# The order of the first column chunks of a fused input projection, and the place of two loads

## The chip, the cores and the metric

One core of one Trainium2 chip. The metric is the device time of one execution in microseconds (us). A core has TensorE (PE in the profile; its weight loads are PEld), VectorE (DVE), ScalarE (ACT), GpSimd (POOL) and SyncE (SP), and 16 DMA engines that serve the queues of SP and POOL. Each engine works through its own instructions in order.

## The reference

One layer of a decoder trunk in float32 with 256 tokens and model width 2048. Three sub-layers, each followed by a LayerNorm of the scaled residual: a hybrid token mixer, a cross-attention into 256 memory tokens, and a SwiGLU feed-forward network. The change lies in the mixer:

```python
gdn_qkv, gdn_gate, gdn_beta, gdn_alpha, ret_qkvg, rwkv_in = jnp.split(x @ w_in, IN_SPLITS, axis=-1)
y_a = gated_deltanet(...)
y_b = retention(...)
y_c = rwkv7_time_mix(rwkv_in, ...)
y = jnp.concatenate([y_a, y_b, y_c], axis=-1)
return y @ w_out
```

and in it in the RWKV-7 group, 12 heads of 64:

```python
p = p + (p_prev - p) * mu                      # token shift
r, k, v, wd, ad, gd = jnp.split(p, RWKV_SPLITS, axis=-1)
w_log = -jax.nn.softplus(-(w0 + jnp.tanh(wd) @ w_up)) - 0.5
decay = jnp.exp(-jnp.exp(w_log))
a = jax.nn.sigmoid(a0 + ad @ a_up)
g = jax.nn.sigmoid(gd) @ g_up
kk = l2_normalize(heads(k * k_k))
k = k * (1.0 + (a - 1.0) * k_a)
...                                            # S_t = S_{t-1}(diag(w) - kk^T (kk a)) + v k^T, y_t = S_t r_t
return y.reshape(b, t, h * n) * g
```

The RWKV part of `w_in` has 2560 columns: 768 of r, 768 of k, 768 of v, and 256 of the rates' inputs (wd, ad, gd).

## The kernel before

Every large product is made by `gemm`. It goes over column chunks of the weight matrix; for each it loads the 2048 rows in four pieces of 512 rows (`ws`, two buffers, issued on SP at line 171), and splits each piece into a high and a low part, two k tiles at a time: a cast on ACT (`wh`, line 181) and a subtraction on DVE (`wl`, line 182). Each k tile then takes six products on PE (lines 159 to 161, for two blocks of 128 tokens: high by high, high by low, low by high). After the last k tile the chunk goes to a `consume` function, here `take`. The parameter `before` lets `load_x` bring the input x in during the first chunk: it loads 512 columns of x on SP (line 260, four buffers), transposes them on PE (line 138) and splits them the same way.

After each k tile, `gemm` calls `hook`, which is the object `side`: a set of lanes (generators). A lane does a piece of work and yields the number of hook calls after which it goes on. So the side work of RWKV, then of the gated DeltaNet group and of retention, is placed between the products. A scheduler in the build then orders each engine's instructions from this program order and from priorities. Lanes wait for each other by flags (`side.until`).

The program begins with the RWKV projection, in seven chunks: the 256 columns of the rates first, then two chunks of 384 for k, two for r and two for v. `take` evacuates each: copies to `nat` (line 389), PE transposes (`wt`, line 399), copies into `buf` (443) and the token shift on DVE (445, 447). For the rates it then applies tanh and sigmoid and adds the lane `from_keys`. That lane first makes the decays of both halves (`decays`, products `lr` at line 486, a scan at 498), then the keys of both halves (`keys`, from line 510, each half as soon as its flag `k0` or `k1` is up), then runs `delta`: the products `aab` into `AT` (line 601), the inverse of 24 triangular systems (`invert`: transposes at 313, a loop of 31 steps of two DVE instructions at 321 and 323, then transposes, copies and small products), with the scores (line 630, which copy under the mask `mask3` at 632) between, and the rest of the recurrence. `from_r` and `from_v` are lanes of their own, added when a chunk of r or v is evacuated; `from_r` sets the flag `r0` or `r1`, which the scores wait for, and ends in the products `pn` (line 406). After the seven chunks `side.run` calls the lanes until both halves of v are done; what is left of `delta` goes on between the products of the next projection, eight chunks of 384 or 396 columns for the gated DeltaNet group.

Small loads are issued on POOL's queue at the start: constants (`twoh`), `mask3` (192 KB), seven small parameter loads into `prow`, then `g_up` (384 KB) and the two halves of `wa_up` (192 KB each). `mask3` is read first by the scores, `g_up` by the products at line 746, near the end of `delta`. At the end of `delta`'s first allocation POOL clears a part of `AT` (line 594).

Of the kernel before, what the change touches and what calls it, by code (L numbers as in the profile page):

```python
# [19 lines left out]
P = 128  # L20
D = 2048
T = 256
NB = T // P
# [8 lines left out]
WH, WN = 12, 64  # L32
WW = WH * WN
# [7 lines left out]
C_RWKV = C_RET + 4 * RW  # L41
# [55 lines left out]
def tile_kernel(ctx: ExitStack, tc: tile.TileContext, ap: dict, out: bass.AP, dbg=None):  # L97
    nc = tc.nc
# [9 lines left out]
    def pst(name):  # L108
        return pm.tile([P, 512], F32, tag="t", name=name, bufs=2)
# [163 lines left out]

    C = load_consts(p1, "twoh", "twoh")
    mask3 = p1.tile([P, 3 * P], I32, tag="mask3", name="mask3")
    nc.gpsimd.dma_start(mask3, ap["mask3"])
    prow = p1.tile([P, P], F32, tag="prow", name="prow")
    nc.vector.memset(prow, 0.0)
    PR_MU, PR_W0, PR_A0, PR_KK, PR_KA, PR_RK, PR_CONV = 0, 20, 26, 32, 38, 44, 50
# [6 lines left out]
    def transpose_params():  # L286
        pp_ = pst("pp")
        nc.tensor.transpose(pp_[:, :P], prow, ident)
        nc.scalar.copy(prm, pp_[:, :P])

    def par(row, j):
        return prm[:, row + j:row + j + 1]
# [88 lines left out]
    HC = WCT // 2  # L381
    G = WH // 2

    def evac_transposed(ps, n, put):

        nat = []
        for b in range(NB):
            t = p1.tile([P, 384], F32, tag="nat", name="nat", bufs=4)
            nc.scalar.copy(t[:, :n], ps[b][:, :n])
            nat.append(t)  # L390
        transposed([t for t in nat], n // P, put)

    def transposed(nat, nt, put, js=None):
        for j in js if js is not None else range(0, nt, 2):
            w = min(2, nt - j)
            pt = pst("wt")
            for i in range(w):
                for b in range(NB):
                    nc.tensor.transpose(pt[:, i * T + b * P:i * T + b * P + P], nat[b][:, (j + i) * P:(j + i + 1) * P], ident)  # L399
            put(j, w, pt[:, :w * T].rearrange("p (i t) -> p i t", t=T))  # L400
# [13 lines left out]
    def rwkv(ctx2):  # L414
# [8 lines left out]
        nc.vector.memset(eps[:, 0:1], 1e-12)  # L423
        nc.vector.memset(eps[:, 1:2], 64e-5)
        g_up = wp.tile([P, WW], F32, tag="gup", name="gup")
        nc.gpsimd.dma_start(g_up, ap["rwkv_g_up"][0])
        gdt = wp.tile([P, T], F32, tag="gdt", name="gdt")

        wl = ctx3.enter_context(tc.tile_pool(name="wl", bufs=1, reuse_waits="tile"))
# [9 lines left out]
        def shifted(dsts, ct0):  # L439
            def put(j, w, pt):  # L440
                buf = wr.tile([P, 2, T + 1], F32, tag="buf", name="buf", bufs=2)
                nc.gpsimd.memset(buf[:, :, 0:1], 0.0)
                nc.scalar.copy(buf[:, :w, 1:], pt)
                d = wr.tile([P, 2, T], F32, tag="dsh", name="dsh", bufs=1)
                nc.vector.tensor_sub(d[:, :w], buf[:, :w, 0:T], buf[:, :w, 1:])
                for i in range(w):
                    nc.vector.scalar_tensor_tensor(dsts[j + i], d[:, i, :], par(PR_MU, ct0 + j + i), buf[:, i, 1:], ALU.mult, ALU.add)
            return put
# [12 lines left out]
        def take(ci, n, ps, bs):  # L461
            if ci == 0:
                transpose_params()
                evac_transposed(ps, n, shifted([wad, gdt], 3 * WCT))
                nc.scalar.activation(wad[0:64], wad[0:64], AF.Tanh)
                nc.scalar.activation(gdt, gdt, AF.Sigmoid)
                side.add(from_keys())
                return
            which, hf = order[ci - 1]
            t = wr.tile([P, HC, T], F32, tag=f"rkv{which}", name=f"rkv{which}", bufs=2 if which == 1 else 1)  # L470
            evac_transposed(ps, n, shifted([t[:, i] for i in range(HC)], which * WCT + hf * HC))
            if which == 1:
                key[hf] = t
                side.flag(f"k{hf}")
            else:
                side.add((from_r if which == 0 else from_v)(hf, t))
# [69 lines left out]
        def from_keys():  # L546
            yield 1
            yield from decays(0)
            yield from decays(1)
            for hf in range(2):  # L550
                yield from side.until(f"k{hf}")
                yield from keys(hf)
            ctx3.close()
            yield from delta(ctx2, RA, KB, vn, bon, fx, eps, g_up, gdt)
# [25 lines left out]
                yield 1  # L580
            side.flag(f"v{hf}")

        order = [(1, 0), (1, 1), (0, 0), (0, 1), (2, 0), (2, 1)]
        chunks = [(C_RWKV + 3 * WW, 256)] + [(C_RWKV + i * WW + hf * HC * P, HC * P) for i, hf in order]
        gemm(xT, w_in, chunks, take, before=load_x, hook=side)
        side.run("v0", "v1", "b0", "b1")
        ctxw.close()

    def delta(ctx2, RA, KB, vn, bon, fx, eps, g_up, gdt):
# [1 line left out]

        ws_ = ctx2.enter_context(tc.tile_pool(name="ws_", bufs=1, reuse_waits="tile"))
        AT = ws_.tile([P, 32, P], F32, tag="AT", name="AT")
        nc.gpsimd.memset(AT[:, NB * WH:, :], 0.0)
        for b in range(NB):
            for c0 in (0, 3):
                pts = [pst("aab") for _ in range(2)]
# [435 lines left out]
    def retention(ctx2):  # L1033
# [67 lines left out]
        for b in range(NB):  # L1101
# [9 lines left out]
            nc.vector.tensor_mul(y_b[:, b], y_b[:, b], yn)  # L1111

    rwkv(ctx.enter_context(ExitStack()))
    ctxr = ExitStack()
    rawp = ctxr.enter_context(tc.tile_pool(name="rawp", bufs=1, side="right", reuse_waits="tile"))
# [219 lines left out]
    with ExitStack() as c2:  # L1335
# [16 lines left out]
        chunks = []  # L1352
# [39 lines left out]
```

## Time and profile before

| | |
|---|---|
| runs shown | 1759.27, 1766.21, 1766.76 us (median 1766.21) |
| profiled execution | 1768.92 us, of which the profiled span 1767.1 us |
| busy share of PE, DVE, ACT, POOL | 98%, 59%, 46%, 4% |
| mean granted TensorE clock | 0.989 of full speed |
| HBM read, rate over the span | 300.63 MB, 171 GB/s |
| mask load, issue to landing | 6.3 us |
| g_up load, issue to landing | 6.0 us |
| first pieces of `ws`, 512 KB, issue to landing (median) | 6.9 us |

The table gives the whole execution. The busy share of PE contains products that run at a lower granted clock and products that wait inside a pipelined stretch, so a stage must also be read by its length against the number of products in it. Row views by window give, for each engine, busy us and the number of instructions, then the granted clock, the busy share of the DMA engines and GB/s. A row of the timeline gives start, length, engine, line, operation, output and inputs, and in brackets the idle time before it and what ended it.

### The profile page before, as it was taken

What the parts mean: (1) busy time and instruction counts of PE and PEld (TensorE: products, weight loads), DVE (VectorE), ACT (ScalarE), POOL (GpSimd) and SP (SyncE); (2) the same over time, 40 slices, a digit from 0 to 9 for tenths busy, and PEclk for the clock granted to TensorE, in tenths of its full rate; (3) what the DMA queues carried; (4) which work ended last, traced back from release to release, by engine and by line L of the source; (5) the groups of instructions that cost most, each with busy time, mean ns of one, the idle gap of its engine ahead of it and who ended that gap; (6) DMA issues with size and microseconds to landing.
All of it is one profiled execution on the core that took longest, in us unless ns stands there. A gap on an engine that the chain in (4) does not pass through costs nothing.

```text
span 1767.1 us, 22057 instructions
## 1 busy us (share of the span) xinstructions
PE 1726.0 (98%) x8853; PEld 1438.1 (81%) x8853; DVE 1035.8 (59%) x1473; ACT 806.8 (46%) x1087; POOL 64.8 (4%) x89
## 2 busy tenths in 40 slices
PE   7999999999999999999999999999999999999997
PEld 6878899898788788877888778888888888888885
DVE  4779357675489655566555755544445554444445
ACT  5633536764444454345543544444444444333342
POOL 2010010000000000011000110000000000000000
PEclk9979999999999999999999999999999999999999
DMA  6433235555544535745445555555555555555553
GB/s 208 144 108 108 92 110 164 161 191 177 180 167 167 190 121 177 273 169 191 143 144 167 188 193 191 190 191 191 190 190 186 187 187 185 185 190 190 191 190 120
DMA packets 158006, 304.15 MB, mean 172 GB/s; under 512 B 5449, under 2 KB 36226, under 8 KB 157136
## 3 DMA queue, kind: packets, MB, share of 16 engines
q1 hardware_dynamic: 156800, 300.01, 50.2%
q0 software_dynamic: 1104, 2.74, 0.6%
q8 instruction: 69, 1.13, 0.3%
q14 instruction: 33, 0.27, 0.0%
HBM read 300.63 MB, written 2.10 MB: 171 GB/s over the span
## 4 chain that ended last, share of the span: by engine, by line
PE 86%; DVE 9%; ACT 2%; issue 1%; DMA 1%; POOL 0%; ACTq 0%; DVEq 0%; POOLq 0%
PE g L159 26%; PE g L160 25%; PE g L161 25%; DVE wl L182 3%; ACT wh L181 1%; PE pt L127 1%; DMA ws<-in_w_in_dram 1%; DVE solX L323 1%; DVE solT L321 1%; DVE res L1238 1%; PE pt L138 1%; DVE solL L313 1%; PE wt L399 1%; PE py L754 1%; PE pn L406 0%
## 5 line engine op out<-in xcount | busy, mean ns | idle before, releaser
L182 DVE TENSOR_TENSOR wl<-ws,wh 128x1024 fp32r<-128x1024 f32 (+2 forms) x560 | 653.0, 1169 | 613.6 <-ACT wh L181 612.9
L181 ACT CAST wh<-ws 128x1024 fp32r<-128x1024 f32 (+2 forms) x560 | 559.5, 1003 | 729.8 <-PE g L161 638.9
L161 PE MATMUL g<-wh,x2T 128*128 128x512 f32 x692 | 271.4, 392 | 0.0
L159 PE MATMUL g<-wh,x2T 128*128 128x512 f32 x692 | 269.7, 390 | 0.0
L160 PE MATMUL g<-wl,x2T 128*128 128x512 f32 x692 | 269.6, 390 | 0.0
L159 PE MATMUL g<-wh,xT 128*128 128x384 f32 (+3 forms) x608 | 219.3, 361 | 0.8 <-ACT wh L181 0.8
L160 PE MATMUL g<-wl,xT 128*128 128x384 f32 (+3 forms) x608 | 217.0, 357 | 0.0
L161 PE MATMUL g<-wh,xT 128*128 128x384 f32 (+3 forms) x608 | 214.3, 352 | 0.0
L160 PEld LDWEIGHTS g<-wl,x2T 128*128 128x128 f32 x692 | 129.9, 188 | 27.3
L159 PEld LDWEIGHTS g<-wh,x2T 128*128 128x128 f32 x692 | 130.1, 188 | 26.4
L161 PEld LDWEIGHTS g<-wh,x2T 128*128 128x128 f32 x692 | 129.9, 188 | 26.1
L161 PE MATMUL g<-wh,hT 128*128 128x512 f32 x336 | 133.1, 396 | 0.0
L159 PE MATMUL g<-wh,hT 128*128 128x512 f32 x336 | 132.9, 396 | 0.0
L160 PE MATMUL g<-wl,hT 128*128 128x512 f32 x336 | 132.9, 395 | 0.0
L159 PEld LDWEIGHTS g<-wh,xT 128*128 128x128 f32 x608 | 117.2, 193 | 10.9 <-issue 2.6
L160 PEld LDWEIGHTS g<-wl,xT 128*128 128x128 f32 x608 | 117.2, 193 | 10.8 <-issue 4.2
L161 PEld LDWEIGHTS g<-wh,xT 128*128 128x128 f32 x608 | 117.1, 193 | 6.4 <-issue 1.5
L159 PE MATMUL g<-wh,mT 128*128 128x512 f32 x256 | 104.8, 409 | 0.0
L160 PE MATMUL g<-wl,mT 128*128 128x512 f32 x256 | 100.5, 393 | 1.6 <-DVE wl L182 1.6
L161 PE MATMUL g<-wh,mT 128*128 128x512 f32 x256 | 100.6, 393 | 0.0
L160 PEld LDWEIGHTS g<-wl,hT 128*128 128x128 f32 x336 | 63.2, 188 | 15.2
L161 PEld LDWEIGHTS g<-wh,hT 128*128 128x128 f32 x336 | 63.2, 188 | 15.2
(450 smaller groups left out, 2157.7 us busy)
## 6 DMA issues: line engine op xcount, KB each, us to landing
ws<-in_ffn_gate_up_dram SPq DMA_DIRECT2D x88, 1024.0 KB, 4.8
ws<-in_ffn_down_dram SPq DMA_DIRECT2D x44, 1024.0 KB, 5.0
ws<-in_w_in_dram SPq DMA_DIRECT2D x52, 768.0 KB, 4.2
ws<-in_w_in_dram SPq DMA_DIRECT2D x16, 1024.0 KB, 4.9
ws<-in_xattn_v_dram SPq DMA_DIRECT2D x16, 1024.0 KB, 5.0
ws<-in_xattn_k_dram SPq DMA_DIRECT2D x16, 1024.0 KB, 5.0
ws<-in_w_out_dram SPq DMA_DIRECT2D x16, 1024.0 KB, 5.1
ws<-in_xattn_q_dram SPq DMA_DIRECT2D x16, 1024.0 KB, 5.0
```

What stands on the lines that cost most here:

```text
L127: nc.tensor.transpose(pt[:, (n % 2) * P:(n % 2 + 1) * P], src(kt), ident)
L138: nc.tensor.transpose(pt[:, k * T + b * P:k * T + b * P + P], src(b, 2 * g + k), ident)
L159: nc.tensor.matmul(ps[b][:, :n], xh, wh, start=(k == 0), stop=False)
L160: nc.tensor.matmul(ps[b][:, :n], xh, wl, start=False, stop=False)
L161: nc.tensor.matmul(ps[b][:, :n], xl, wh, start=False, stop=(k == nk - 1))
L181: nc.scalar.copy(wh[:, :, :n], ws[:, 2 * k2:2 * k2 + 2, :n])
L182: nc.vector.tensor_sub(wl[:, :, :n], ws[:, 2 * k2:2 * k2 + 2, :n], wh[:, :, :n].bitcast(F32))
L313: nc.vector.transpose(L[p], at[p, :, p].rearrange("p s t -> p t s"))
L321: nc.vector.tensor_tensor(t, X[:, m:m + 1, 0:nj].to_broadcast([P, ni, nj]), L[:, m + 1:32, m:m + 1].to_broadcast([P, ni, nj]), ALU.mult)
L323: nc.vector.tensor_tensor(X[:, m + 1:32, 0:nj], X[:, m + 1:32, 0:nj], t, ALU.add)
L399: nc.tensor.transpose(pt[:, i * T + b * P:i * T + b * P + P], nat[b][:, (j + i) * P:(j + i + 1) * P], ident)
L754: nc.tensor.matmul(o, l, r, start=(start and n == 0), stop=(stop and n == len(ops) - 1))
```

## The change

The order of the first two chunks is exchanged: 384 columns of k (first half) come first, with x's loads beside them, and the 256 columns of the rates second. In `take`, the transposition of the parameter rows stays with the first chunk, the rates' evacuation and the start of the lane `from_keys` go to the second. The loads of `mask3` and `g_up` are no longer issued at the start but on POOL's queue directly behind the clearing of `AT` in `delta`; `tc.issue_after` fixes that order on the queue.

```diff
     mask3 = p1.tile([P, 3 * P], I32, tag="mask3", name="mask3")
-    nc.gpsimd.dma_start(mask3, ap["mask3"])
...
         g_up = wp.tile([P, WW], F32, tag="gup", name="gup")
-        nc.gpsimd.dma_start(g_up, ap["rwkv_g_up"][0])
...
         def take(ci, n, ps, bs):
             if ci == 0:
                 transpose_params()
+            if ci == 1:
                 evac_transposed(ps, n, shifted([wad, gdt], 3 * WCT))
                 nc.scalar.activation(wad[0:64], wad[0:64], AF.Tanh)
                 nc.scalar.activation(gdt, gdt, AF.Sigmoid)
                 side.add(from_keys())
                 return
-            which, hf = order[ci - 1]
+            which, hf = order[ci]
...
-        order = [(1, 0), (1, 1), (0, 0), (0, 1), (2, 0), (2, 1)]
-        chunks = [(C_RWKV + 3 * WW, 256)] + [(C_RWKV + i * WW + hf * HC * P, HC * P) for i, hf in order]
+        order = [(1, 0), None, (1, 1), (0, 0), (0, 1), (2, 0), (2, 1)]
+        chunks = [(C_RWKV + x[0] * WW + x[1] * HC * P, HC * P) if x else (C_RWKV + 3 * WW, 256) for x in order]
...
-        nc.gpsimd.memset(AT[:, NB * WH:, :], 0.0)
+        with tc.issue_after(nc.gpsimd.memset(AT[:, NB * WH:, :], 0.0).ins):
+            nc.gpsimd.dma_start(mask3, ap["mask3"])
+            nc.gpsimd.dma_start(g_up, ap["rwkv_g_up"][0])
```

## The prediction

> **What bounds the kernel now.** I read the page first: how busy TensorE (PE) is, and where in the span its share or its clock falls. 40 slices of a 1767 us span are 44.2 us each.
>
> ```profile
> span 1767.1 us, 22057 instructions
> PE 1726.0 (98%) x8853; PEld 1438.1 (81%) x8853; DVE 1035.8 (59%) x1473; ACT 806.8 (46%) x1087; POOL 64.8 (4%) x89
> PE   7999999999999999999999999999999999999997
> PEclk9979999999999999999999999999999999999999
> ```
>
> PE is the bound; only the first slices are thinner, and only the third shows a low clock. The change lives there, in the RWKV input projection. I cut that stretch where its seven column chunks end (each is 96 products of lines 159 to 161; I call the chunks c0 to c6) and add the first chunk after it. Columns: busy time of each engine, granted clock, DMA share, GB/s.
>
> ```profile
> 0.00:25.28 25.28, 17.93 (x129) 17.26 (x129) 10.77 (x20) 10.60 (x18) 9.22 (x24) 1.00 0.83 260
> 25.28:55.32 30.04, 26.36 (x127) 21.59 (x126) 16.92 (x29) 21.26 (x37) 0.10 (x1) 0.89 0.43 141
> 55.32:77.34 22.02, 21.33 (x116) 18.38 (x114) 17.64 (x29) 13.73 (x21) 0.28 (x2) 1.00 0.45 144
> 77.34:106.23 28.89, 28.81 (x140) 24.74 (x138) 20.46 (x30) 10.91 (x18) 5.12 (x5) 0.82 0.34 109
> 106.23:136.07 29.84, 26.01 (x135) 22.43 (x134) 23.29 (x35) 10.68 (x19) 3.06 (x5) 0.83 0.33 106
> 136.07:163.62 27.55, 26.96 (x183) 22.62 (x182) 25.80 (x56) 8.84 (x14) 0.20 (x2) 1.00 0.35 113
> 163.62:187.05 23.43, 22.41 (x207) 20.54 (x206) 21.14 (x41) 12.72 (x21) 0.20 (x2) 1.00 0.43 139
> 187.05:204.50 17.45, 17.45 (x262) 15.82 (x262) 4.40 (x7) 9.70 (x19) 0.00 (x0) 1.00 0.15 47
> ```
>
> Then the timeline of the start and of c1, for the pace of products and the waits inside "busy".
>
> ```profile
> 2.29 0.59 POOL L276 DMA_DIRECT2D mask<-in_mask_dram  x1
> 8.88 0.56 POOL L426 DMA_DIRECT2D gup<-in_rwkv_g_up_dram  x1 [0.88 <-DMA mask<-in_mask_dram]
> 10.02 0.78 PE L159 MATMUL g<-wh,xT 128*128 128x256 f32 x2
> 17.98 1.14 ACT L181 CAST wh<-ws 128x512 fp32r<-128x512 f32 x2 [2.90 <-DMA ws<-in_w_in_dram]
> 20.08 0.28 PE L159 MATMUL g<-wh,xT 128*128 128x256 f32 x1
> 20.20 0.28 PE L160 MATMUL g<-wl,xT 128*128 128x256 f32 x1
> 24.71 1.57 ACT L181 CAST wh<-ws 128x768 fp32r<-128x768 f32 x2 [3.57 <-DMA ws<-in_w_in_dram]
> 26.60 0.33 PE L399 MATMUL wt<-ident,nat 128*128 128x128 f32 x1 [1.20 <-ACT nat L389]
> 27.29 0.35 PE L159 MATMUL g<-wh,xT 128*128 128x384 f32 x1
> 27.47 0.34 PE L160 MATMUL g<-wl,xT 128*128 128x384 f32 x1
> 32.92 0.77 PE L486 MATMUL lr<-wad,waup 64*128 64x256 f32 x4 [1.15 <-ACT wad L465]
> 35.74 1.46 PE L486 MATMUL lr<-wad,waup 64*128 64x256 f32 x4 [1.33 <-ACT sg L488]
> 126.59 1.86 PE L406 MATMUL pn<-rkv,csts_twoh 128*6 128x256 f32 x4 [3.83 <-DVE rkv L565]
> ```
>
> Products start 0.12 us apart at 256 columns and 0.17 to 0.18 at 384, so a 384 chunk is worth about 16.6 us and a 256 chunk 11.5. The table shows c1 to c6 at 22 to 30 us: the RWKV side work and waits behind it take the rest. The granted clock falls three times there:
>
> ```profile
> 36.00:40.00 4.00, 4.00 (x12) 2.30 (x12) 0.80 (x2) 1.84 (x5) 0.00 (x0) 0.53 0.61 195
> 40.00:44.00 4.00, 4.00 (x16) 4.00 (x16) 3.42 (x9) 2.42 (x3) 0.00 (x0) 0.61 0.01 2
> 92.00:100.00 8.00, 8.00 (x29) 6.20 (x28) 6.15 (x9) 0.83 (x1) 1.23 (x2) 0.64 0.52 182
> 100.00:108.00 8.00, 8.00 (x45) 7.07 (x44) 1.64 (x2) 4.37 (x10) 3.64 (x2) 0.72 0.00 0
> 124.00:132.00 8.00, 5.41 (x15) 2.94 (x16) 6.54 (x17) 0.53 (x2) 0.00 (x0) 0.56 0.61 197
> 132.00:140.00 8.00, 8.00 (x41) 7.47 (x39) 5.06 (x11) 4.22 (x7) 0.00 (x0) 0.80 0.10 22
> ```
>
> By one minus the clock, times the window, these dips cost 3.4, 5.1 and 5.1 us.
>
> **The change, part by part.**
>
> *Loads taken from the start.* The mask (192 KB) and g_up (384 KB) go: 0.59 MB. The DMA engines move up to 374 GB/s there:
>
> ```profile
> 8.00:12.00 4.00, 2.71 (x13) 2.74 (x14) 2.48 (x4) 1.80 (x4) 1.92 (x7) 1.00 1.09 374
> ws<-in_w_in_dram SPq DMA_DIRECT2D x52, 768.0 KB, 4.2
> ```
>
> That is 1.6 us of DMA time. Removing both also takes two issues of 0.6 us off POOL's queue and lets the two loads of wa_up behind them go sooner.
>
> *A wider first chunk.* Each of its four weight loads grows from 512 to 768 KB, 0.26 MB or 0.7 us. The third load (its cast waits 2.90 us for it now) has 0.79 MB more and 0.59 less ahead of it: it lands 0.5 us later; the fourth 1.2 us later. Between first product and third load lie 48 products, 8.3 us instead of 5.8, so PE needs it 2.5 us later: covered, and the fourth too. The first product itself has no cover: load +0.7, cast and subtraction a half longer (1.14 us for two casts now, so about +0.3 each for one), mask's 0.5 us gone: between 0 and +1.3; I take +0.8.
>
> *The next chunk's loads.* Today c1's first cast waits 3.57 us for DMA, and PE 1.20 us for `nat`, a copy behind that cast on ACT. In the new order the 256-column loads are asked for while 384-column products still run (4.2 us per load against 24 x 0.173 = 4.15 us of products, two buffers). The wait goes: -1.2 (PE's own), bounds 0 and -3.6 (ACT's). What is late next is the same `nat` copy without DMA ahead of it.
>
> *Order of RWKV's side work.* I counted its steps (one per product pair of k). The decays start after the rates' chunk, now second: they move from c1 to c2, keys(0) from c2 to c3, keys(1) from the first ten steps of c3 to the end of c3 and five of c4; the inverse begins 11 steps later (c4 step 9, before c3 step 14), its 31-step loop ends at c6 step 16 instead of 5, and RWKV ends in the fourth instead of the third chunk of the next projection. That projection has 128 steps, and the group behind it ends at the same step in both orders. PE's side work is the same; what counts is what it lies beside. The waits of 1.15 and 1.33 us and the table loads behind them move with the decays: 0. Only the 256-column chunk now carries no decays.
>
> DVE decides c4 to c6 (25.80 of 27.55 us in c5). Rows of DVE's groups, first of the stretch 25 to 106, then 106 to 205:
>
> ```profile
> L182 DVE TENSOR_TENSOR wl<-ws,wh 128x768 fp32r<-128x768 f32 x27 | 25.4, 949 | 18.4 <-ACT wh L181 18.3
> ...
> L313 DVE STREAM_TRANSPOSE solL<-AT 32x1024 f32<-32x1024 f32 x4 | 8.1, 2018 | 2.0 <-ACT AT L604 1.9
> ...
> L331 DVE COPY AT<-AT 32x768 f32<-32x768 f32 x4 | 2.2, 546 | 0.1
> L326 DVE STREAM_TRANSPOSE solL<-solX 128x1024 f32<-128x1024 f32 x1 | 2.1, 2136 | 0.0
> L328 DVE STREAM_TRANSPOSE AT<-solX 128x1024 f32<-128x1024 f32 x1 | 2.0, 2003 | 0.0
> ```
>
> Eight weight subtractions are 7.6 us a chunk. c2 and c3 together hold 17.6 + 20.5 - 15.2 = 22.9 us of other DVE work, 11.4 for each half of the keys. New c3 gets one and a half halves: 7.6 + 17.1 = 24.7 us, against 22.0 us that c2 takes with 17.6 of DVE: +2.7. Out of c6 go the last transposes and copies, 2.1 + 2.0 + 2.2 = 6.3 us, into a chunk that has room (4.40 of 17.45); into c4 to c6 come half of the keys' work, about 5: -1.3. The wait of 3.83 us on `rkv`, behind transposes of 2.0 us each, should leave the r half that runs before them now and return at the second, which runs right after: 0, bounds -8.9 and +8.9 (wait and dip gone, or one of each added). Keys no longer needed the moment they arrive: -1 (0 to -2).
>
> *Mask and g_up later.* Issued behind POOL's clearing of AT, some ten steps before the scores read the mask: 0.59 MB beside weight loads at a DMA share of 0.33. Cost 0 to +1.6, I take +0.3. Queued behind them on POOL are only memsets of AT and `sc`, needed later still.
>
> *Dips.* Nothing removes their causes; they are short pauses whose timing shifts. Any of the three, 3.4 to 5.1 us, may go, or a fourth come. As c1 no longer combines late loads and decays, I count a third of a mean dip as gone: -1.5.
>
> Sum: +0.8 - 1.2 + 2.7 - 1.3 - 1 + 0.3 - 1.5 = -1.2; I round to -2 for POOL's and `wa_up`'s earlier issue. The profiled execution took 1768.9 (span plus 1.8), 2.7 above the median of the runs; -2 gives 1767 there and about 1764 as a median.
>
> [...] The dip at 36 us follows PE waits of 1.15 and 1.33 us, and in the window at 92 PE is busy for all of its 8.00 us; so here short pauses go with losses of 3 to 5 us, more than themselves, and moved waits are priced with dips. [...]
>
> **Rivals.**
> 1. *Dips go.* Two of the three do not recur: 3.4 + 5.1 to 5.1 + 5.1, so -8.5 to -10.2 on top of -0.5 of the rest: 1756. For it: they follow pauses whose place all shifts, and the fastest run shown, 1759.27, is 7 us below the others. Against: all waits that lead to them stay in the kernel.
> [...]
> 3. *DVE becomes the bound of c3 and c4 (slower).* c4 would hold 7.6 + half the keys 5 + 8.1 of transposes + the r half's shifts and products, about 5, so 25.7; a chunk with 25.8 took 27.55. If c3 behaves likewise: +5.5 on c2's 22.0; c4 +2.8 over its 29.84 less its 5.1 dip; and a starved PE brings one dip more, 5.1: +13 less 2: 1777. It decides once DVE's work in a chunk passes the 23 us or so that PE needs. For it: DVE runs in order, so PE's `wl` waits behind RWKV. Against: today's sums come near it only in c5.
> 4. *The first chunk arrives too late*: the bound +1.3 plus fourth load uncovered 1.2, nothing gained behind: about +2, 1768; no change.
>
> **How the numbers follow.** A measurement here tells about 0.5%, 8.8 us, from no change. Forecast with case 4 (1758 to 1771): 0.62. Rivals 1 and 2: 0.15 and 0.07. Rival 3: 0.14. The remaining 0.02 lies in faster mixes. So faster 0.24, same 0.62, slower 0.14. The range takes in rival 1's far end and most of rival 3: 1752 to 1775.
>
> **What will show it.** Right: no mask or g_up issue before the AT clearing; first product near 10.8; PE dense until c0 ends near 31 and c1 near 44, without a DMA wait of ACT over 1 us between; decays beside c2; end of c6 near 180 to 186. Wrong: weight waits on DVE throughout c3 and c4, a gap of PE over 2 us in the first 31, or a different count of stretches with a clock under 0.8.

## The result, and the profile after

Nine runs of the changed kernel took 1770.04 to 1787.83 us, median 1773.45; nine of the kernel before 1759.27 to 1766.76, median 1764.43. The ratio is 1.008, 95% interval 1.006 to 1.0099: slower by 14 us by this ratio, by 9.0 by the medians; three of the nine runs, at 1785.63 to 1787.83, make most of the difference between the two. The forecast was 1764, no change.

The page of the profile after (its execution took 1773.45 us): PE is as busy as before, the low clock sits in other slices. The profiled execution of before, 1768.92 us, is slower than each of before's nine runs.

```profile
span 1771.7 us, 22047 instructions
PE 1730.1 (98%) x8853; PEld 1441.1 (81%) x8853; DVE 1034.8 (58%) x1473; ACT 806.3 (46%) x1087; POOL 64.9 (4%) x89
PEclk9998799999999999999999999999999999999999
```

The seven chunks again, cut where 96 products end, and then a stretch of delta's tail (columns as in the prediction; each cut lies one product late, so that the last product of c0 ended at 31.4, of c1 at 43.9, of c4 at 117.6 us):

```profile
0.00:31.88 31.88, 24.27 (x133) 23.23 (x134) 15.19 (x23) 14.74 (x22) 8.13 (x22) 1.00 0.72 229
31.88:44.03 12.15, 12.15 (x103) 11.94 (x102) 7.42 (x12) 5.90 (x12) 0.20 (x2) 1.00 0.57 174
44.03:71.75 27.72, 25.65 (x125) 21.05 (x126) 16.51 (x30) 21.13 (x34) 0.10 (x1) 0.94 0.45 143
71.75:93.03 21.28, 21.25 (x116) 18.48 (x115) 18.46 (x30) 12.41 (x21) 0.37 (x2) 1.00 0.41 128
93.03:119.06 26.03, 26.03 (x142) 21.08 (x140) 20.21 (x31) 11.68 (x20) 6.17 (x7) 1.00 0.48 161
119.06:156.89 37.83, 33.31 (x213) 27.93 (x213) 29.61 (x55) 10.58 (x20) 3.05 (x5) 0.86 0.26 84
156.89:175.61 18.72, 18.34 (x109) 17.61 (x110) 18.24 (x38) 9.17 (x15) 0.20 (x2) 1.00 0.45 139
175.61:221.69 46.08, 45.03 (x454) 40.25 (x454) 19.51 (x37) 20.13 (x35) 0.00 (x0) 0.78 0.26 83
```

The seven chunks end at 175.6 us, 11 us ahead of before. The loss comes behind them. Before, the stretch from 176 to 204, where most of the inverse's small products ran, had the full clock (first row); after, 4 us windows of the same work (the others):

```profile
176.00:204.00 28.00, 27.05 (x385) 24.30 (x383) 13.58 (x19) 15.76 (x28) 0.00 (x0) 1.00 0.27 86
```

```profile
192.00:196.00 4.00, 4.00 (x83) 3.51 (x81) 1.54 (x2) 1.91 (x5) 0.00 (x0) 1.00 0.52 189
196.00:200.00 4.00, 4.00 (x78) 3.78 (x77) 0.00 (x0) 1.60 (x4) 0.00 (x0) 0.73 0.00 0
200.00:204.00 4.00, 4.00 (x74) 3.56 (x73) 0.00 (x0) 0.82 (x2) 0.00 (x0) 0.50 0.02 4
204.00:208.00 4.00, 4.00 (x27) 3.38 (x24) 0.98 (x1) 1.44 (x3) 0.00 (x0) 0.50 0.00 0
208.00:212.00 4.00, 4.00 (x23) 3.44 (x23) 0.00 (x0) 0.73 (x2) 0.00 (x0) 0.50 0.62 203
212.00:216.00 4.00, 4.00 (x22) 3.44 (x23) 0.00 (x0) 1.35 (x3) 0.00 (x0) 0.50 0.00 0
216.00:220.00 4.00, 4.00 (x27) 3.40 (x26) 0.98 (x1) 1.36 (x3) 0.00 (x0) 0.71 0.02 4
```

By one minus the clock, 10.2 us are lost, and PE is "busy" in all of it. The timeline of PE just ahead shows with what: groups of 24 to 48 products of 32 x 32 (`pu`) and 12 of 128 x 64 (`pav`, the right-hand sides), with six, three and two full products (those of `gemm`) between (189.97 to 191.11, 193.36 to 194.08, 195.61 to 196.16).

```profile
187.74 0.94 PE L755 MATMUL pu<-solL,AT 32*32 32x32 f32 x24 [0.66 <-DVE solL L325]
188.61 1.55 PE L755 MATMUL pav<-vn,sc 128*128 128x64 f32 x12
189.97 0.42 PE L159 MATMUL g<-wh,xT 128*128 128x384 f32 x1
...
191.11 1.45 PE L755 MATMUL pav<-vn,sc 128*128 128x64 f32 x12
192.49 0.94 PE L755 MATMUL pu<-solL,AT 32*32 32x32 f32 x24
193.36 0.44 PE L159 MATMUL g<-wh,xT 128*128 128x384 f32 x1
...
194.08 1.60 PE L755 MATMUL pu<-solL,AT 32*32 32x32 f32 x48
195.61 0.44 PE L159 MATMUL g<-wh,xT 128*128 128x384 f32 x1
...
199.14 0.52 PE L159 MATMUL g<-wh,xT 128*128 128x384 f32 x1
199.46 0.52 PE L160 MATMUL g<-wl,xT 128*128 128x384 f32 x1
```

Before, twelve full products stood between the second group of `pu` (at 180.01 us) and the third, twelve more ahead of `pn`, and `pav` came only behind the inverse's first three stages:

```profile
183.17 1.60 PE L754 MATMUL pu<-solL,AT 32*32 32x32 f32 x48
186.98 0.84 PE L754 MATMUL pn<-solX,AT 32*32 32x32 f32 x21
199.01 1.55 PE L754 MATMUL pav<-vn,sc 128*128 128x64 f32 x12
```

Cut at its edges, the stretch after lasts 20.48 us, six times 3.41, and the 3.41 us ahead of it had PE busy throughout:

```profile
194.45:197.86 3.41, 3.41 (x105) 3.12 (x102) 0.00 (x0) 1.01 (x3) 0.00 (x0) 1.00 0.02 5
197.86:218.34 20.48, 20.48 (x171) 17.81 (x169) 1.97 (x2) 6.19 (x11) 0.00 (x0) 0.50 0.13 41
```

In windows of 0.25 us, all 41 dips in the first 400 us of the 13 profiles last one, two, three, four or six times 3.41 us at 0.50 (in before 6.83, 10.24 and 10.24 us, in after 3.41, 10.24, 20.48 and 3.41), and within one profile their starts lie whole numbers of 3.41 us apart. So in these profiles the clock is granted in steps of 3.41 us, a low step costs 1.7 us, and the grid of steps lies differently from execution to execution (in before a step begins 2.1 us behind the span's start, in after 3.3, in after again 3.0).

One sum ties the runs together: span times mean clock. Before 1767.1 x 0.989 = 1747.7; after 1771.7 x 0.987 = 1748.7; over the nine runs of after, whose clocks go from 0.978 to 0.990, it is 1746 to 1751 while the times differ by 18 us (the clock has three digits, so each product is good to 0.9 us). By this sum the two kernels would take the same time at full clock; what the change moves is how long PE is granted half of it.

### The profile page after: what moved, and what is told of

It is laid out like the page before. It is cut to its first block, busy times and chain, and to the rows that moved or that the text cites. A ratio compares the mean times of both kernels' runs of the same rounds, so it can differ in the third digit from the quotient of the medians.

```text
span 1771.7 us, 22047 instructions
## 1 busy us (share of the span) xinstructions
PE 1730.1 (98%) x8853; PEld 1441.1 (81%) x8853; DVE 1034.8 (58%) x1473; ACT 806.3 (46%) x1087; POOL 64.9 (4%) x89
## 4 chain that ended last, share of the span: by engine, by line
PE 86%; DVE 8%; DMA 3%; ACT 2%; issue 1%; POOL 0%; SPq 0%; ACTq 0%; DVEq 0%; POOLq 0%
PE g L159 25%; PE g L161 25%; PE g L160 25%; DVE wl L182 3%; DMA ws<-in_w_in_dram 2%; ACT wh L181 1%; PE pt L127 1%; DVE solL L312 1%; DVE res L1239 1%; DMA xs<-in_x_dram 1%; DVE solX L322 1%; DVE solT L320 1%; PE pn L405 1%; PE py L755 1%; PE wt L398 1%
```

## The experiments

I call this theory A: delta, begun 11 steps later, has its inverse's small products at a worse place, and the clock falls there. Rivals: B, the later loads; C, DVE over-full; D, the wide first chunk or late decays themselves; E and F on the dip's cause.

| kernel | median, us | range, us | ratio to before, 95% interval | profiled span, us | clock | span x clock |
|---|---|---|---|---|---|---|
| loads only | 1762.41 | 1757.26 to 1763.67 | 0.9989, 0.9978 to 0.9999 | 1758.3 | 0.995 | 1749.5 |
| order only | 1782.26 | 1770.90 to 1786.86 | 1.0086, 1.0057 to 1.0116 | 1771.6 | 0.987 | 1748.6 |
| before, delta 11 later | 1775.17 | 1771.92 to 1778.65 | 1.0066, 1.0042 to 1.0091 | 1770.2 | 0.988 | 1749.0 |
| after, inverse spread | 1769.92 | 1763.13 to 1773.69 | 1.0019, 0.9999 to 1.0040 | 1771.9 | 0.987 | 1748.9 |
| the same, rhs behind | 1764.96 | 1760.88 to 1771.04 | 1.0021, 1.0005 to 1.0036 | 1759.1 | 0.996 | 1752.1 |
| after, delta 11 earlier | 1764.56 | 1761.07 to 1780.80 | 1.0028, 0.9999 to 1.0058 | 1760.3 | 0.993 | 1748.0 |
| after, keys denser | 1770.67 | 1762.69 to 1772.59 | 1.0030, 1.0015 to 1.0045 | 1768.6 | 0.989 | 1749.1 |
| after, bonus later | 1770.33 | 1768.01 to 1774.19 | 1.0050, 1.0032 to 1.0069 | 1768.4 | 0.988 | 1747.2 |
| loads only, bonus later | 1784.70 | 1764.22 to 1786.32 | 1.0084, 1.0045 to 1.0123 | 1763.7 | 0.991 | 1747.8 |
| after, filled | 1776.88 | 1775.21 to 1781.16 | 1.0075, 1.0059 to 1.0091 | 1775.1 | 0.991 | 1759.1 |
| after again | 1770.92 | 1770.22 to 1785.90 | 1.0074, 1.0040 to 1.0108 | 1768.4 | 0.988 | 1747.2 |

**Loads only.** The diff's three edits on `mask3` and `g_up`, nothing of `order` or `take`.

> Only the loads of mask and g_up move behind the clearing of AT; the chunk order stays as before. Theory A (the loss is granted clock, above all from about 198 to 219 us, where the small products of RWKV's inverse stand close together in the next projection's first chunk because delta begins 11 steps later): this kernel keeps the old place of the inverse, so no dip near 200 us and a time within 3 us of before (about 1764). Theory B (the later mask and g_up loads delay weight loads or the scores): all or most of the +9 us shows here, 1771 to 1774. Theory C (DVE is over-full in c4 to c6 by the compacted side work): as before, 1764.

1762.41 us, 0.1% faster. B falls. It is the fastest kernel of all.

**Order only.** The edits on `order`, `chunks` and `take`; both loads at the start.

> Only the chunk order changes; mask and g_up are loaded at the start. A: as after, 1770 to 1778, with the clock at about half between about 198 and 219 us. B: as before, 1764, if the loads are the cause; if the crowded start is what they were moved away from, the first chunk ends 2 us later than after's 31.9. C: as after, with DVE over 95% in c5 and c6.

As after, 1.0086, with the same windows at half clock. The last product of its first chunk ended at 31.2 us against 31.4 in after, so the loads at the start held nothing up.

**The kernel before, delta later.**

```diff
             ctx3.close()
+            yield 11
             yield from delta(ctx2, RA, KB, vn, bon, fx, eps, g_up, gdt)
```

> The kernel before with one edit: the lane waits 11 more steps before delta, so that the inverse lies where after has it; chunk order and loads as before. A: a dip of the clock at some 190 to 225 us, worth about 10 us, comes with it: 1770 to 1778. B: 1764, since start and loads are untouched. C: slower by some us too, but with the loss in c5 and c6 at full clock.

1.0066, with the old chunk order and loads: eleven empty steps make most of the loss. I cut the rest of each span in stages: from the end of the seven chunks to the end of the third chunk of the next projection (first row), and the next five chunks (second row); the second column is the length. Before, then loads only:

```profile
187.05:288.80 101.75, 101.75 (x934) 94.62 (x934) 48.76 (x120) 41.76 (x70) 10.69 (x16) 1.00 0.35 108
288.80:384.36 95.56, 95.45 (x550) 89.13 (x549) 70.37 (x153) 69.31 (x104) 1.23 (x10) 1.00 0.52 168
```

```profile
178.00:279.74 101.74, 101.74 (x933) 94.62 (x934) 48.76 (x120) 41.15 (x69) 10.69 (x16) 1.00 0.36 107
279.74:376.49 96.75, 95.93 (x549) 89.17 (x549) 70.31 (x153) 70.11 (x104) 1.22 (x10) 1.00 0.55 166
```

After, and after again:

```profile
175.61:288.59 112.98, 111.93 (x1022) 103.30 (x1022) 51.53 (x119) 41.89 (x72) 5.98 (x9) 0.91 0.31 98
288.59:390.62 102.03, 99.79 (x558) 91.09 (x557) 77.06 (x180) 72.20 (x109) 6.03 (x17) 0.98 0.52 163
```

```profile
175.61:288.58 112.97, 111.86 (x1022) 103.24 (x1022) 51.61 (x119) 41.89 (x72) 5.98 (x9) 0.91 0.32 98
288.58:387.68 99.10, 98.17 (x558) 90.58 (x557) 77.03 (x180) 72.38 (x109) 6.02 (x17) 1.00 0.56 167
```

Before with delta later:

```profile
176.06:288.38 112.32, 111.14 (x1021) 102.78 (x1022) 49.58 (x110) 41.97 (x72) 6.00 (x9) 0.92 0.33 98
288.38:388.78 100.40, 98.16 (x558) 90.56 (x557) 76.98 (x180) 72.14 (x109) 6.02 (x17) 1.00 0.55 165
```

First stage: 101.7 us at full clock, or 112.3 to 113.0 at 0.91 to 0.92; by one minus the clock, 9 to 10 of the 11 us are clock. Second stage: 95.6 and 96.8, or 99.1 to 102.0. Here the gated DeltaNet group's lane, begun 11 steps later, has 7 us more of DVE work in the same chunks, which goes with 2.4 to 6.5 us more; in the first profile of after a wait of 2.24 us and a short dip are part of it. From there to the end the kernels differ by 2 us at most.

The rows also show that after's lead of 11 us at the end of c6 is mostly not its merit: loads only, with the old order, is there at 178.0, as the half-clock stretch that before's profile had from 92 to 108 us did not recur in it.

**The kernel after, inverse spread; and the right-hand sides behind it.** In `invert`, after the loop, `yield gap` with 3 in place of `yield 1`; the second kernel also has

```diff
             yield from side.until("v0", "v1")
-            rhs(0)
...
         yield from first
+        rhs(0)
+        yield 1
```

> The kernel after with one edit: in RWKV's inverse, after the loop of 31 steps, each step of small products yields 3 instead of 1, so that 18 instead of 6 large products lie between two groups. A: the dip from 198 to 219 us goes or shrinks to under 3 us: 1760 to 1765. B: no change, 1773. C: no change in c5 and c6; at most 2 us.

> The kernel with the spread inverse, and the right-hand sides of the first token block (24 small products into pav) moved behind the inverse, so that the first group of the inverse stands alone among large products. A: the half-clock stretch that began right behind the first group and pav (192 to 208 us, 5.7 us) goes: 1762 to 1767, against 1770 for the spread alone. Rival E (the dip belongs to the wait for the transposed inverse on DVE, 0.67 us, before the first group): it stays, 1770.

The spread alone shortened the half-clock stretch to 13.7 us, 6.8 us lost (the second expectation counted 5.7): less than A asked for, as it now began behind the first `pu` group and `pav`. With `pav` moved away it was gone in the profile. Windows of the first and the second kernel:

```profile
192.00:208.00 16.00, 16.00 (x120) 14.84 (x120) 5.06 (x8) 4.64 (x9) 0.00 (x0) 0.57 0.21 57
208.00:224.00 16.00, 16.00 (x209) 15.39 (x208) 4.92 (x5) 7.97 (x13) 0.00 (x0) 1.00 0.46 147
```

```profile
192.00:208.00 16.00, 16.00 (x227) 15.11 (x225) 5.90 (x6) 8.22 (x14) 0.00 (x0) 1.00 0.42 121
208.00:224.00 16.00, 16.00 (x119) 15.02 (x117) 4.81 (x5) 7.31 (x12) 0.00 (x0) 1.00 0.42 134
```

1769.92 and 1764.96 us, ratios 1.0019 and 1.0021: with delta as late as in after, most of the loss comes back when the small products are thinned out. What moving `pav` adds rests on the two profiles, and these are of the slowest of six runs and of the fastest of ten; four of the ten still took 1768.97 to 1771.04, at 0.990 to 0.991. Rival E falls: the wait of 0.66 us before the first group is still there, and no dip follows it.

**The kernel after, delta earlier, two ways.** First, the decays' six inner steps per half yield 0 (and the lane's first step 2); second, the keys' yields 1, 1, 1, 0, 1, 0 in place of 2, 1, 2, 1, 1, 1.

> The kernel after with delta begun 11 steps earlier, where before has it: the decays of both halves yield nothing between their three column tiles. Chunk order and loads are those of after. Theory A (the loss is granted clock, caused by where delta's inverse lies): no half-clock stretch near 198 to 219 us, 1758 to 1766; another dip beside the now denser decays (50 to 70 us) may cost 3 to 5 us of that. Rival D (the wide first chunk or the late decays are themselves the cause): stays at 1771 to 1778 although delta is early.

> The kernel after with delta begun 12 steps earlier by another way: each half of the keys takes 4 instead of 10 steps, while the decays keep theirs. A: no half-clock stretch at 190 to 220 us, and none of the 5 us that the denser decays cost at 52 to 64: 1757 to 1763, as good as the loads alone or a little better. Rival D (the wide first chunk itself costs): 1770 or more. If DVE is over-full by the denser keys: a longer c3 (over 24 us) at full clock, 1764 to 1768.

The first had seven of ten runs at 1761 to 1766 and three at 1778 to 1781; in its profile, of the run at 1762.14, the stretch up to the third chunk's end took 107.39 us, with one short dip (186.8 to 190.2), and a dip of 5.1 us lay beside the denser decays, as expected. D falls: the wide first chunk and the late decays can go with 1762. The second missed: 1770.67, and its profile shows the stretch at half clock although delta is early:

```profile
188.00:196.00 8.00, 8.00 (x115) 7.43 (x114) 1.44 (x3) 3.16 (x7) 0.00 (x0) 0.50 0.05 16
196.00:204.00 8.00, 8.00 (x53) 6.56 (x52) 0.68 (x1) 2.60 (x5) 0.00 (x0) 0.50 0.01 2
204.00:212.00 8.00, 8.00 (x65) 7.82 (x63) 0.28 (x1) 1.87 (x4) 0.00 (x0) 0.75 0.33 101
```

Its small products stand close all the same: `pu` at 184.08 and 185.33 and `pn` at 186.56 have one full product between each, and `pav` is not among them. Two of its runs (1762.69, 1764.41, at 0.995 and 0.994) look as if they had escaped the stretch; they were not profiled. So an early delta makes the dip rarer, it does not exclude it; the profiles point to how close the small groups stand, rather than to the step at which delta begins. How the clock goes with the number of full products in a step of 3.41 us was not measured, and which runs fall over is open.

**The kernel after, filled.** Behind each small-product step of RWKV's inverse:

```diff
+        pt = pst("fill").rearrange("p (k t) -> p k t", k=2)
+        for i in range(3):
+            nc.tensor.matmul(pt, xT[0][:, 0, 0, 0:P], xT[0][:, :, 0, :], start=True, stop=True)
```

> The kernel after with added work and nothing else: behind each of the 12 steps of small products in RWKV's inverse come three full products (128 x 128 by 512 columns, about 0.22 us each at full clock, 7.8 us in all) whose result nobody reads. Theory A (the clock falls because too little of the array's full work is done in some microseconds of small products): the half-clock stretch at 196 to 220 us (10.7 us lost) shrinks to under 3 us, so the 7.8 us of added work cost nothing: 1768 to 1774. Rival F (the dip has another cause, such as the wait before the first group or a fixed time): the dip stays and the added work runs partly at half clock: 1781 to 1789.

Between the two: 1776.88. Its full-clock time is 10 us longer than in after's first profile (1759.1), its span only 3.4 us. The stretch lasts 10.2 us instead of 20.5, and 5.1 us are lost instead of 10.2, which pays for about half of the added work:

```profile
196.00:200.00 4.00, 4.00 (x94) 3.59 (x95) 0.00 (x0) 1.49 (x4) 0.00 (x0) 0.81 0.01 4
200.00:204.00 4.00, 4.00 (x53) 3.39 (x51) 0.96 (x1) 1.62 (x3) 0.00 (x0) 0.50 0.02 4
204.00:208.00 4.00, 4.00 (x43) 3.74 (x42) 0.00 (x0) 1.41 (x3) 0.00 (x0) 0.50 0.68 203
208.00:212.00 4.00, 4.00 (x32) 3.68 (x30) 0.98 (x1) 0.85 (x1) 0.00 (x0) 0.91 0.00 0
```

F in its strict form (a fixed time for the whole dip) falls; A's "under 3 us" (5.1 were left) was too hopeful.

**Bonus later.** `yield 8` for `yield 2` ahead of the head sums in `from_r`, on after and on loads only.

> The kernel after with one number changed: the lane of r waits 8 instead of 2 steps between its DVE products and PE's head sums. A: PE's wait of 4.09 us at 136 us and the half-clock stretch from 140 to 152 us (5.0 us) go, the dip at 196 to 220 us stays: 8 to 9 us faster than after, 1764 to 1769. If a wait costs only itself: 4 us faster, 1769. If DVE is what bounds that stretch: no gain, 1773.

> The kernel before with only the loads moved and the lane of r waiting 8 steps. A: its dip at 116 to 124 us (1.7 us) and the wait ahead of it (about 4 us) go: 1755 to 1759, about 5 us faster than the loads alone (1762.4). If DVE bounds that stretch: 1762.

Both missed. On after the wait on `rkv` left and one on the inverse's loop took its place; on loads only it stayed. Timeline of PE, first and second kernel:

```profile
139.82 2.26 PE L631 MATMUL ps<-RA,KB 64*128 64x128 f32 x12 [2.10 <-DVE solT L320]
```

```profile
120.23 2.72 PE L405 MATMUL pn<-rkv,csts_twoh 128*6 128x256 f32 x6 [3.82 <-DVE rkv L563]
```

DVE was busy for 10.00 of the 10 us from 130 in the first and 10.88 of the 11 us from 110 in the second, so DVE bounds that stretch, and this is where C holds. Loads only with this edit had runs in two groups, four at 1764 to 1765 and six at 1785 to 1786, the upper one unprofiled; its clocks were 0.978 to 0.980 against 0.991 to 0.993.

**After again.**

> The kernel after, unchanged, for a second profile. Its times fall into two groups, 1770 to 1777 and 1785 to 1788. A: whichever group this one is in, its span times its mean clock is 1746 to 1751 us; in the upper group some 15 us more lie in half-clock stretches. Otherwise the upper group has the same clock as the lower and a longer stretch of waits.

Its profile is of the lower group (1770.22) and repeats the stretch at 0.50 to the window. That the upper group is clock too rests on the clocks of the runs: the three at 1785.63 to 1787.83 had 0.978 to 0.981, and two more here, at 1783.04 and 1785.90, 0.980 and 0.981. Where in the span those 15 us lie was not seen.

## Why the prediction was wrong, point by point

- **The start: right in the main.** c0 was forecast to end near 31 and c1 near 44; measured 31.4 and 43.9. The first product came at 9.72 us, not 10.8: the +0.8 was -0.3. One DMA wait of ACT over 1 us remained (1.60, third load), with PE still fed. PE's wait of 1.20 us for `nat` at the second chunk went, as forecast; one of 0.52 us came at the third. The end of c6 was forecast at 180 to 186; it came at 175.6, and loads only, without the new order, had 178.0.
- **Loads moved: right.** Mask and g_up were issued at 113.9 and 114.5 us, behind the clearing of `AT` at 113.0; loads only shows no cost.
- **DVE in c3: wrong.** +2.7 was forecast; the chunk took 21.28 us, 0.7 less than c2 before, with 18.46 us of DVE work, not 24.7: it held one half of the keys, not one and a half, and the second half ran in c4, up to 114.6 us. c5, with 29.61 us of DVE work, took 37.83 us, with the wait of 4.09 us and its dip at the second r half. That the wait would move there was the prediction's "0", and it was right.
- **The step that failed** is "PE's side work is the same; what counts is what it lies beside", which left the later tail out of the sum, at 0; the next projection was looked at only as "a chunk that has room". Room for work it has; but the same small products, with fewer full ones between, cost 9 to 10 us of clock in both profiles of after and in before with delta later. The prediction tied dips to short pauses of PE, and looked for them only in the seven chunks; this one came without a pause.
- **The same step, smaller:** "the group behind it ends at the same step in both orders" leaves out that the group starts later: the five chunks in which it catches up took 2.4 to 6.5 us more, with 7 us more DVE work in them. That the one makes the other was not tested by itself.
- **Dips: sign wrong.** -1.5 assumed that fewer would come. In the lower group of runs the result is in the main one more, larger one: 10.2 us. The direction of rival 3 came true by another mechanism, not by DVE in c3 and c4, and that the median lies inside 1752 to 1775 is luck: the range was wide enough for rival 3, not for this.
- **What the clock did.** It fell at 197.86 us behind 3.41 us in which PE was busy by the profile (3.41 of 3.41), with no wait over 0.66 us near, so no longer pause went ahead of it here, and it stood at 0.50 for 20.48 us. The steps of 3.41 us lie on a grid that starts elsewhere from execution to execution, 2.1 us behind the span's start in before, 3.3 in after, 3.0 in after again.
- **The chance of 0.07 for rival 2.** No run shows what it rests on; what the runs showed in its place is this fall with PE busy, and the wait on `rkv` again, 4.09 us, with a dip of 10.24 us (139.84 to 150.07 us) in c5.

## What to carry to other kernels

Before comparing two orders of the same work, multiply span by mean granted clock: if the products agree (here 1747 to 1750 us in ten of the kernels, 1752 in the one with the right-hand sides behind), next to nothing but clock was won or lost, and the place to look is the windows under 1.00. Work made of many tiny products should not be bunched where full ones are at hand: thinning it out brought the ratio from 1.008 to 1.002 here. Keeping other tiny work (here `pav`) from falling between may help further; one profile suggests it, the times do not show it. The best kernel found keeps the old chunk order and moves only the two loads, 0.9989 of before, so the useful part of the change is small and its order should be undone.

## What the runs showed of the hardware

- PE at half clock behind 3.41 us in which it was busy all the time (194.45 to 197.86 us), with products of 32 x 32 and two full ones among them. In the stretch at 0.50 full products ran 0.32 us apart instead of 0.17, and the clock came back only after 20.5 us.
- The clock changed on a grid of 3.41 us, whose place differs from execution to execution (2.1, 3.3 and 3.0 us behind the span's start): all 41 dips of the first 400 us in the 13 profiles are whole numbers of steps long, at 1.7 us lost in each step.
- Runs of one kernel in two groups, some 10 to 20 us apart, told by their mean clocks: after 0.985 to 0.990 and 0.978 to 0.981, order only 0.987 to 0.988 and 0.979 to 0.982, loads only with the bonus later 0.991 to 0.993 and 0.978 to 0.980. The same program can fall on either side; whether the place of the grid decides it was not tested.
